# An encoder trunk: products of zeros on TensorE ahead of the first weights, and the state-space matrices fetched earlier

## The chip, the cores and the metric

One Trainium2 chip, one core of it. The metric is the device time of one execution in microseconds. Names of engines: TensorE is PE (its weight loads are PEld), VectorE is DVE, ScalarE is ACT, GpSimd is POOL, and SyncE is SP, whose queue only issues transfers here.

## The reference

A two-layer encoder on 256 tokens of width 1024, all in float32. Each layer adds half a SwiGLU block, a mixer of three branches and half a SwiGLU block again; a norm ends the trunk.

```python
for i in range(DEPTH):                                   # 2 layers
    h = rms_norm(x, ffn1_norm[i])
    x = x + 0.5 * (silu(h @ w_gate) * (h @ w_up)) @ w_down   # 1024 -> 2816 -> 1024
    h = rms_norm(x, mix_norm[i])
    ... = split(h @ w_in[i])                             # columns of three branches
    y_s5   = s5_branch(u, lambda, log_dt, b, c, d, w_glu)    # state space: bu = B_bar u, scan, C
    y_gla  = gla_branch(...)                             # gated linear attention
    y_attn = attn_branch(...)                            # attention with rotary positions
    gates  = sigmoid(h @ w_merge_gate[i] + b_merge_gate[i])
    x = x + (sum of gates * (y @ w_branch)) @ w_out[i]
    h = rms_norm(x, ffn2_norm[i])
    x = x + 0.5 * swiglu_ffn(h, ...)
return rms_norm(x, final_norm)
```

The state-space branch has complex matrices B and C (s5_b_re, s5_b_im, s5_c_re, s5_c_im; 2 directions, 32 groups, 64 states, 16 channels). Tables for it are made from B, C and the parameters lambda and log_dt.

## The kernel before

**Weights.** Every large product runs as three products of float32r parts (`mm3`, lines 234 to 236): the activation's high part by the weight's high part, by the weight's low part, and its low part by the weight's high part. `load` fetches weights in tiles of 128 x 2 x 512 (512 KB; for the gate and up matrices SP issues one transfer each, line 220), ScalarE casts the tile to hi (line 224), and VectorE subtracts to lo (line 225). The tiles `raw` rotate through 5 buffers, and so do hi and lo. The small vector tiles of `vectors` take a buffer of the `raw` ring too. A `raw` buffer is free again when its lo is made.

**Streaming.** `stream` walks over blocks of 512 output columns and chunks of 4 k-tiles (2 weight tiles). In `ffn` the first two blocks go side by side: step 0 is block 0 with the first chunk, step 1 block 1 with the first chunk, step 2 block 0 with the second, step 3 block 1 with the second, then two steps to a block. A weight tile is used by 12 products of 128x128 by 512 columns (2 k-tiles, 2 token tiles, 3 parts). The very first chunk is loaded in finer pieces (one k-tile each, `fine`).

**The norm.** `Norm.half` transposes half of x on TensorE (line 1158) and makes its high and low parts hTh and hTl; `ffn` calls `half(0)` ahead of the stream, and the hook of step 0 makes `half(1)`. In `__init__` x and the vector ffn1_norm are fetched first, with high priority; `vectors` transposes the vector (line 189).

**The tables.** `s5_tables` is a generator that `weave` interleaves with the feed-forward stream: in layer 0 from step 2 on with 1.8 of its parts to a step (PREP), in layer 1 from step 6 on with 0.85. Its first part fetches cst, three vectors (layer 0) and tcst. Then come `s5_params` (lambda as lm, log_dt as ld, lines 420 and 421, and some 17 parts of small VectorE work), `small_tables` (gla_norm, w_alpha as wraw, attn norms), and then B as bn (line 531, 4 transfers of 128 KB) and C as cn (line 537, 32 transfers of 16 KB in rows of 256 B). cn shares its memory with the scratch tiles U0 and U1, so the trace names it U. TensorE transposes cn (line 543, cT), and the rest builds the tables of four groups q.

**Order.** The program is traced in the order of the code, and a planner (`schedule_with_timeline_sim`) then fixes each engine's queue ahead of time, by its own estimate of when operands and buffers are ready; where several instructions are ready for an engine, the one that was traced first goes first. `high_priority()` without an offset puts instructions to the front; `load` uses it with an offset of 0 (WPRIO), so weight loads stand at their traced place. `behind` adds an order between two instructions of a queue without a wait; cst is tied so behind the last weight load. On the chip each queue is worked off strictly in its order.

Of the kernel before, what the change touches and what calls it, by code (L numbers as in the profile page):

```python
# [9 lines left out]
F32 = mybir.dt.float32  # L10
# [5 lines left out]
P = 128  # L16
# [66 lines left out]
def cols(*parts):  # L83

    def f(a, z):
        res, o = [], 0
        for w, cs in parts:
            res.append((w[a * P:z * P, cs].rearrange("(k p) n -> p k n", p=P), 0, o))
            o += cs.stop - cs.start
        return res  # L90
    return f
# [34 lines left out]
class Enc:  # L126
    def __init__(self, tc, ctx, ins, out):
        self.tc, self.nc, self.ctx, self.ins, self.out = tc, tc.nc, ctx, ins, out
        nc = self.nc
        pool = lambda name, bufs, **kw: ctx.enter_context(tc.tile_pool(name=name, bufs=bufs, **kw))  # L130
        self.const = pool("const", 1)
        self.wraw = pool("wraw", WBUFS[0])
        self.whl = pool("whl", WBUFS[1])
        self.hp = pool("hp", 1)
        self.st = pool("st", 2)
        self.pmm = pool("pmm", 3, space=bass.MemoryType.PSUM)
        self.psm = pool("psm", 3, space=bass.MemoryType.PSUM)
        self.ptr = pool("ptr", 2, space=bass.MemoryType.PSUM)
        self.n = self.ahead_by = 0
        c = self.const  # L140
        self.ident = c.tile([P, P], F32, name="ident")
        make_identity(nc, self.ident)
        self.x = c.tile([P, NT, D], F32, name="x")
        self.cst = c.tile([P, C_MIX], F32, name="cst")
        self.row = {}
        self.mhalf = c.tile([P, 32], F32, name="mhalf")
        nc.gpsimd.memset(self.mhalf, -0.5)

        nc.scalar.activation(c.tile([P, 1], F32, name="warm"), self.mhalf[:, :1], AF.Silu)
        with tc.high_priority():  # L150
            xd = lambda eng, t, h: eng.dma_start(self.x[:, t, h * 512:(h + 1) * 512],
                                                 ins["x"][0, t * P:(t + 1) * P, h * 512:(h + 1) * 512])
            xd(nc.scalar, 0, 0)
            xd(nc.sync, 1, 0)
            self.vectors("ffn1_norm", eng=nc.scalar)
            for t in range(NT):
                xd(nc.scalar, t, 1)
        self.ld = pool("s5ld", 1)
        self.ahead, self.small = {}, {}
        self.scr = {(l, q): tc.dram_tile([P, SCR], F32, name=f"scr{l}_{q}") for l in range(DEPTH) for q in range(NQ)}  # L160
# [4 lines left out]

    def t2(self, shape, dt=F32, ring="ra"):
        return self.phase.tile(shape, dt, name=self.nm("t"), tag=ring, bufs=self.rings[ring])

    def vectors(self, *names, eng=None):

# [108 lines left out]
    def ffn(self, l, which, nm, nxt):  # L279

        nc, ins = self.nc, self.ins
        wg, wu, wd = (ins[f"{which}_w_{s}"][l] for s in ("gate", "up", "down"))
        with self.tc.tile_pool(name=f"ffn{which}{l}", bufs=1) as fp:
            self.phase, self.rings = fp, {"ra": 4}
            if nm.at == 0:
                nm.half(0)
            act, rstd = nm.act, nm.rstd
            sh = fp.tile([P, KF, SEQ], F32R, name=f"sTh{which}{l}")
            sl = fp.tile([P, KF, SEQ], F32R, name=f"sTl{which}{l}")

            def evac(b):
                def f(t, ps):
                    self.n += 1
                    sg, s = self.t2([P, 256]), self.t2([P, 256])
                    nc.scalar.activation(sg, ps[:, :256], AF.Silu, scale=rstd[:, t:t + 1])  # L295
                    nc.vector.scalar_tensor_tensor(s, ps[:, 256:], rstd[:, t:t + 1], sg, op0=ALU.mult, op1=ALU.mult)  # L296
                    pt = self.ptr.tile([P, 2, P], F32, name=f"st{self.n}", tag="tr")
                    for j in range(2):
                        nc.tensor.transpose(pt[:, j], s[:, j * P:(j + 1) * P], self.ident)  # L299
                    h = sh[:, 2 * b:2 * b + 2, t * P:(t + 1) * P]  # L300
                    nc.scalar.copy(h, pt)  # L301
                    nc.vector.tensor_tensor(sl[:, 2 * b:2 * b + 2, t * P:(t + 1) * P], pt, h.bitcast(F32),  # L302
                                            op=ALU.subtract)
                return f

            blocks = []
            for b in range(KF // 2):
                cs = slice(b * 256, (b + 1) * 256)
                blocks.append((cols((wg, cs), (wu, cs)), 512, evac(b)))
            yield from self.stream(act, KD, blocks, lead=2, hooks={0: nm.finish}, fine=(l, which) == (0, "ffn1"))  # L310
            nm2 = self.nxt = nxt()
            last = isinstance(nm2, Final)

            def down(c):
                def f(t, ps):
                    xs = self.x[:, t, c * 512:(c + 1) * 512]
                    nc.vector.scalar_tensor_tensor(xs, ps, 0.5, xs, op0=ALU.mult, op1=ALU.add)
                    if last:
                        nm2.half(c, t)
                return f  # L320

            sact = lambda k, t: (sh[:, k, t * P:(t + 1) * P], sl[:, k, t * P:(t + 1) * P])
            yield from self.stream(sact, KF, [(cols((wd, slice(c * 512, (c + 1) * 512))), 512, down(c))
                                              for c in range(2)],
                                   hooks=() if last else {-(-KF // WCH) + 1: lambda: nm2.half(0)},
                                   tail=3 * WCH if last else None)
# [183 lines left out]
    def s5_tables(self, l, pp):  # L510
        nc, ins = self.nc, self.ins
# [3 lines left out]
            self.vectors("mix_norm", "ffn2_norm", "s5_d")  # L515
        self.tcst = pp.tile([P, C_ALL - C_MIX], F32, name="tcst")
        nc.sync.dma_start(self.tcst, ins["cst"][:, C_MIX:])
        yield
        yield from self.s5_params(l, pp)
        yield  # L520
        self.small_tables(l, pp)
        yield
        b = []
        T2 = [pp.tile([P, GQ, 64], F32, name=f"U{i}") for i in range(4)]
        cn = [T2[i].rearrange("p g c -> p (g c)").rearrange("p (t r) -> p t r", t=4) for i in range(2)]
# [1 line left out]
        for i, s in enumerate(("re", "im")):  # L527
            bn = pp.tile([P, G, 16], F32, name=self.nm("bn"))
            b.append(bn)
            for d in range(2):  # L530
                nc.sync.dma_start(bn[d * 64:(d + 1) * 64], ins[f"s5_b_{s}"][l, d].rearrange("g p f -> p g f"))
            for d in range(2):
                for e in range(2):
                    for h in range(2):
                        for ii in range(2):
                            r = e * 64 + h * 32 + ii * 16
                            nc.sync.dma_start(
                                cn[i][r:r + 16, :, d * 64:(d + 1) * 64],
                                ins[f"s5_c_{s}"][l, d].rearrange("(h q i e) f p -> e h i f q p", q=NQ, e=2, h=2)[e, h, ii])
        for i in range(2):  # L540
            ps = self.psm.tile([P, 4, P], F32, name=self.nm("cT"), tag="sm")
            for t in range(4):
                nc.tensor.transpose(ps[:, t], cn[i][:, t], self.ident)
            nc.scalar.copy(cq[:, i], ps)
            if i == 1:
                nc.scalar.activation(cq[:, 2], ps, AF.Copy, scale=-1.0)
        yield
        T = [pp.tile([P, GQ, 4, 16], F32, name=f"T{i}") for i in range(4)]
        for q in (1, 2, 3, 0):
# [14 lines left out]
            for i in range(2):  # L564
                ps = self.psm.tile([P, 4, P], F32, name=self.nm("bT"), tag="sm")
# [15 lines left out]
            for i in range(2):  # L581
                for a in range(4):
                    for d in range(2):
# [3 lines left out]
                                         start=i == 0, stop=i == 1)  # L587
# [545 lines left out]
class Norm:  # L1133
# [14 lines left out]
        return self.hi[:, k, ts], self.lo[:, k, ts]  # L1148

    def half(self, c):  # L1150
        e, nc = self.e, self.e.nc
        self.at = c + 1
        for j in range(2):
            pt = e.ptr.tile([P, 2, SEQ], F32, name=e.nm("pt"), tag="tr")
            for i in range(2):
                k = 4 * c + 2 * j + i
                for t in range(NT):
                    nc.tensor.transpose(pt[:, i, t * P:(t + 1) * P], e.x[:, t, k * P:(k + 1) * P], e.ident)
            for i in range(2):
                k = 4 * c + 2 * j + i  # L1160
                g, h = self.g[:, k:k + 1], self.hi[:, k]
                nc.scalar.activation(h, pt[:, i], AF.Copy, scale=g)  # L1162
                nc.vector.scalar_tensor_tensor(self.lo[:, k], pt[:, i], g, h.bitcast(F32), op0=ALU.mult, op1=ALU.subtract)
        for t in range(NT):
            nc.scalar.activation(e.t2([P, 512]), e.x[:, t, c * 512:(c + 1) * 512], AF.Square,
                                 accum_out=self.sq[:, c, t:t + 1])

    def finish(self):
        e, nc = self.e, self.e.nc
# [89 lines left out]
```

## Time and profile before

| | |
|---|---|
| Median of 3 runs | 1335.75 us (1334.98 to 1336.29) |
| Profiled execution | 1336.15 us, span of its instructions 1334.4 us |
| TensorE products | 1299.3 us busy, 97% of the span |
| VectorE, ScalarE, GpSimd | 75%, 52%, 6% of the span |
| Transfers | 249.87 MB, mean 187 GB/s |

The profile is of one execution; times in it count from the start of its span. Products are pipelined: one that is shown with 0.39 us can follow the one before it after 0.23 us, so the distance of starts tells the pace. A row of the time axis that ends in x2 or more merges instructions of one kind that follow each other. A bracket at its end says how long the engine was idle before it and what ended that.

### The profile page before, as it was taken

To read this page: it belongs to the slowest core of one execution; us is meant where nothing else is said; L and a number is where in the kernel's file an instruction comes from. 1 tells how busy PE (TensorE), PEld (TensorE's weight loads), DVE (VectorE), ACT (ScalarE), POOL (GpSimd) and SP (SyncE) were. 2 spreads that over 40 slices of the span, in tenths; PEclk is the share of its full clock that TensorE was granted. 3 is DMA by queue.
4 is the path that set the end of the run, shared out by engine and by line. 5 is a ranking of instruction groups with operands and counts; after the bars stand their busy time and mean duration, and the time that the engine had idled before them with its cause. 6 is when DMAs were issued, how large, how long until landed. Compare 5 with 4: busy or idle time off the path is not lost.

```text
span 1334.4 us, 19260 instructions
## 1 busy us (share of the span) xinstructions
PE 1299.3 (97%) x6792; PEld 1049.9 (79%) x6792; DVE 1001.1 (75%) x1798; ACT 699.8 (52%) x1132; POOL 81.2 (6%) x109
## 2 busy tenths in 40 slices
PE   8999999999999999999999999999999999999997
PEld 6788878878787777888888778887787867788886
DVE  5899896789996778997576757557899966655553
ACT  6454455547685445544454454463485853655442
POOL 1022211000100000101010000000001000000000
PEclk9999999999999999999999999999999999999999
DMA  8775686765463457677656565576655525555661
GB/s 254 180 216 162 228 299 193 208 230 192 155 195 111 127 162 198 193 250 233 189 168 210 180 221 182 172 201 203 193 192 185 177 65 173 165 181 186 194 204 63
DMA packets 201264, 249.87 MB, mean 187 GB/s; under 512 B 40920, under 2 KB 134664, under 8 KB 201168
## 3 DMA queue, kind: packets, MB, share of 16 engines
q1 hardware_dynamic: 200416, 247.33, 59.5%
q8 instruction: 53, 0.87, 0.3%
q10 hardware_dynamic: 752, 1.32, 0.3%
q14 instruction: 43, 0.35, 0.1%
HBM read 234.44 MB, written 13.11 MB: 186 GB/s over the span
## 4 chain that ended last, share of the span: by engine, by line
PE 74%; DVE 13%; DMA 5%; issue 4%; POOL 2%; SPq 1%; ACT 1%; POOLq 0%; ACTq 0%; DVEq 0%
PE mm L234 22%; PE mm L236 22%; PE mm L235 22%; DVE lo L225 3%; DMA e<-scr 2%; DMA raw<-in_ffn_w_up 2%; DVE t L330 2%; POOL kx L610 1%; PE st L299 1%; DVE run L823 1%; PE as L1057 1%; PE ao L1079 1%; PE S L805 1%; DVE run L822 1%; ACT hi L224 1%
## 5 line engine op out<-in xcount | busy, mean ns | idle before, releaser
L225 DVE TENSOR_TENSOR lo<-raw,hi 128x1024 fp32r<-128x1024 f32 (+2 forms) x414 | 498.9, 1209 | 190.3 <-ACT hi L224 184.5
L224 ACT CAST hi<-raw 128x1024 fp32r<-128x1024 f32 (+2 forms) x414 | 428.6, 1039 | 339.5 <-PE mm L236 271.4
L234 PE MATMUL mm<-hi,hTh 128*128 128x512 f32 (+1 forms) x1120 | 441.2, 396 | 4.9 <-ACT hTh L1162 2.6
L235 PE MATMUL mm<-lo,hTh 128*128 128x512 f32 (+1 forms) x1120 | 440.8, 395 | 3.3 <-DVE lo L225 3.0
L236 PE MATMUL mm<-hi,hTl 128*128 128x512 f32 (+1 forms) x1120 | 431.0, 392 | 0.0
L234 PEld LDWEIGHTS mm<-hi,hTh 128*128 128x128 f32 x1120 | 211.5, 189 | 48.6 <-ACT hTh L1162 3.1
L235 PEld LDWEIGHTS mm<-lo,hTh 128*128 128x128 f32 x1120 | 211.3, 189 | 45.4 <-DVE lo L225 5.1
L236 PEld LDWEIGHTS mm<-hi,hTl 128*128 128x128 f32 x1120 | 210.9, 189 | 40.9
L235 PE MATMUL mm<-lo,sThffn 128*128 128x512 f32 x352 | 137.6, 391 | 0.9 <-DVE lo L225 0.9
L236 PE MATMUL mm<-hi,sTlffn 128*128 128x512 f32 x352 | 137.5, 392 | 0.0
L234 PE MATMUL mm<-hi,sThffn 128*128 128x512 f32 x352 | 136.5, 393 | 0.7 <-ACT hi L224 0.7
L235 PEld LDWEIGHTS mm<-lo,sThffn 128*128 128x128 f32 x352 | 66.1, 188 | 15.1 <-DVE lo L225 1.6
L234 PEld LDWEIGHTS mm<-hi,sThffn 128*128 128x128 f32 x352 | 66.1, 188 | 14.6 <-ACT hi L224 1.1
L236 PEld LDWEIGHTS mm<-hi,sTlffn 128*128 128x128 f32 x352 | 66.1, 188 | 14.2
L295 ACT ACTIVATE t<-mm,rstd 128x256 f32<-128x256 f32 x88 | 41.2, 474 | 52.8 <-PE mm L236 50.7
L301 ACT CAST sThffn<-st 128x256 fp32r<-128x256 f32 x88 | 31.4, 372 | 68.5 <-PE st L299 68.1
L302 DVE TENSOR_TENSOR sTlffn<-st,sThffn 128x256 fp32r<-128x256 f32 x88 | 35.7, 417 | 35.5 <-ACT sThffn L301 35.5
L296 DVE SCALAR_TENSOR_TENSOR t<-mm,rstd,t 128x256 f32<-128x256 f32 x88 | 40.7, 477 | 11.7 <-ACT t L295 11.5
L610 POOL COPY kx<-ks 128x128 f32<-128x128 f32 x32 | 28.1, 919 | 231.0 <-DVE ks L593 187.0
L299 PE MATMUL st<-ident,t 128*128 128x128 f32 x176 | 31.7, 274 | 1.6 <-DVE t L296 0.8
L299 PEld LDWEIGHTS st<-ident,t 128*128 128x128 f32 x176 | 23.4, 140 | 11.9 <-DVE t L296 1.3
L330 DVE TENSOR_TENSOR t<-e,S 128x512 f32<-128x512 f32 x32 | 20.3, 682 | 15.1 <-DMA e<-scr 12.5
(355 smaller groups left out, 1411.5 us busy)
## 6 DMA issues: line engine op xcount, KB each, us to landing
raw<-in_ffn_w_down SPq DMA_DIRECT2D x88, 512.0 KB, 4.6
raw<-in_ffn_w_gate SPq DMA_DIRECT2D x174, 256.0 KB, 2.8
raw<-in_ffn_w_up SPq DMA_DIRECT2D x174, 256.0 KB, 3.8
raw<-in_w_in SPq DMA_DIRECT2D x48, 512.0 KB, 4.9
raw<-in_w_merge_gate SPq DMA_DIRECT2D x48, 512.0 KB, 4.5
raw<-in_w_out SPq DMA_DIRECT2D x16, 512.0 KB, 4.9
scr<-e SPq DMA_DIRECT2D x6, 768.0 KB, 8.2
e<-scr SPq DMA_DIRECT2D x6, 768.0 KB, 6.4
```

The costliest lines, as they stand in the source:

```text
L224: nc.scalar.copy(hi[:, j:z, :width], raw[:, j:z, :width])
L225: nc.vector.tensor_tensor(lo[:, j:z, :width], raw[:, j:z, :width], hi[:, j:z, :width].bitcast(F32), op=ALU.subtract)
L234: nc.tensor.matmul(ps, act[0], w[0], start=first, stop=False)
L235: nc.tensor.matmul(ps, act[0], w[1], start=False, stop=False)
L236: nc.tensor.matmul(ps, act[1], w[0], start=False, stop=last)
L295: nc.scalar.activation(sg, ps[:, :256], AF.Silu, scale=rstd[:, t:t + 1])
L296: nc.vector.scalar_tensor_tensor(s, ps[:, 256:], rstd[:, t:t + 1], sg, op0=ALU.mult, op1=ALU.mult)
L299: nc.tensor.transpose(pt[:, j], s[:, j * P:(j + 1) * P], self.ident)
L301: nc.scalar.copy(h, pt)
L302: nc.vector.tensor_tensor(sl[:, 2 * b:2 * b + 2, t * P:(t + 1) * P], pt, h.bitcast(F32), op=ALU.subtract)
L330: self.nc.vector.tensor_tensor(out, a, b, op=ALU.mult)
L610: nc.gpsimd.tensor_copy(kx[:, :, s], ks.rearrange("p g j f -> p g (j f)")[:, :, (3 - s) * 16:(3 - s) * 16 + 64])
```

## The change

A tile of zeros is made on VectorE. `idle(n)` issues n products of this tile with itself (128x128, float32) into a PSUM tile of the ring `mm` that nobody reads. 11 of them are traced at the head of `__init__`, with high priority, and 8 in the first `ffn`, each behind the last transpose of `half(0)`, which now returns it. In `s5_tables` the fetches of B and C are moved from behind `small_tables` to the first part, behind tcst; the transposes of C stay where they were. The number of parts is the same.

```diff
--- before.py
+++ after.py
@@ -147,7 +147,11 @@
         nc.gpsimd.memset(self.mhalf, -0.5)
 
         nc.scalar.activation(c.tile([P, 1], F32, name="warm"), self.mhalf[:, :1], AF.Silu)
+
+        self.zero = c.tile([P, P], F32, name="zero")
+        nc.vector.memset(self.zero, 0.0)
         with tc.high_priority():
+            self.idle(11)
             xd = lambda eng, t, h: eng.dma_start(self.x[:, t, h * 512:(h + 1) * 512],
                                                  ins["x"][0, t * P:(t + 1) * P, h * 512:(h + 1) * 512])
             xd(nc.scalar, 0, 0)
@@ -165,6 +169,14 @@
 
     def t2(self, shape, dt=F32, ring="ra"):
         return self.phase.tile(shape, dt, name=self.nm("t"), tag=ring, bufs=self.rings[ring])
+
+    def idle(self, n, prev=None):
+
+        ps = self.pmm.tile([P, 512], F32, name=self.nm("idle"), tag="mm")
+        for _ in range(n):
+            m = self.nc.tensor.matmul(ps[:, :P], self.zero, self.zero, start=True, stop=True)
+            if prev is not None:
+                self.behind(m, prev)
 
     def vectors(self, *names, eng=None):
 
@@ -283,7 +295,7 @@
         with self.tc.tile_pool(name=f"ffn{which}{l}", bufs=1) as fp:
             self.phase, self.rings = fp, {"ra": 4}
             if nm.at == 0:
-                nm.half(0)
+                self.idle(8, nm.half(0))
             act, rstd = nm.act, nm.rstd
             sh = fp.tile([P, KF, SEQ], F32R, name=f"sTh{which}{l}")
             sl = fp.tile([P, KF, SEQ], F32R, name=f"sTl{which}{l}")
@@ -515,11 +527,6 @@
             self.vectors("mix_norm", "ffn2_norm", "s5_d")
         self.tcst = pp.tile([P, C_ALL - C_MIX], F32, name="tcst")
         nc.sync.dma_start(self.tcst, ins["cst"][:, C_MIX:])
-        yield
-        yield from self.s5_params(l, pp)
-        yield
-        self.small_tables(l, pp)
-        yield
         b = []
         T2 = [pp.tile([P, GQ, 64], F32, name=f"U{i}") for i in range(4)]
         cn = [T2[i].rearrange("p g c -> p (g c)").rearrange("p (t r) -> p t r", t=4) for i in range(2)]
@@ -537,6 +544,11 @@
                             nc.sync.dma_start(
                                 cn[i][r:r + 16, :, d * 64:(d + 1) * 64],
                                 ins[f"s5_c_{s}"][l, d].rearrange("(h q i e) f p -> e h i f q p", q=NQ, e=2, h=2)[e, h, ii])
+        yield
+        yield from self.s5_params(l, pp)
+        yield
+        self.small_tables(l, pp)
+        yield
         for i in range(2):
             ps = self.psm.tile([P, 4, P], F32, name=self.nm("cT"), tag="sm")
             for t in range(4):
@@ -1148,6 +1160,7 @@
         return self.hi[:, k, ts], self.lo[:, k, ts]
 
     def half(self, c):
+
         e, nc = self.e, self.e.nc
         self.at = c + 1
         for j in range(2):
@@ -1155,7 +1168,7 @@
             for i in range(2):
                 k = 4 * c + 2 * j + i
                 for t in range(NT):
-                    nc.tensor.transpose(pt[:, i, t * P:(t + 1) * P], e.x[:, t, k * P:(k + 1) * P], e.ident)
+                    last = nc.tensor.transpose(pt[:, i, t * P:(t + 1) * P], e.x[:, t, k * P:(k + 1) * P], e.ident)
             for i in range(2):
                 k = 4 * c + 2 * j + i
                 g, h = self.g[:, k:k + 1], self.hi[:, k]
@@ -1164,6 +1177,7 @@
         for t in range(NT):
             nc.scalar.activation(e.t2([P, 512]), e.x[:, t, c * 512:(c + 1) * 512], AF.Square,
                                  accum_out=self.sq[:, c, t:t + 1])
+        return last
 
     def finish(self):
         e, nc = self.e, self.e.nc
```

## Rows read from the trace of the kernel before

**Rows 1.** The page, busy time: us (share of span) x instructions

```profile
PE 1299.3 (97%) x6792; PEld 1049.9 (79%) x6792; DVE 1001.1 (75%) x1798; ACT 699.8 (52%) x1132; POOL 81.2 (6%) x109
```

**Rows 2.** Waits of TensorE, whole span: us in total, times, longest

```profile
PE mm L235 <- DVE lo L225: 3.9, 3, 1.5
...
PE cT L543 <- DMA U<-in_s_c_re: 0.7, 1, 0.7
...
PE cT L543 <- DMA U<-in_s_c_im: 0.3, 1, 0.3
```

**Rows 3.** Time axis of the opening: start, duration, engine, line, output<-input

```profile
5.71 1.97 PE L1158 MATMUL pt<-ident,x 128*128 128x128 f32 x8
...
8.46 1.22 PE L234 MATMUL mm<-hi,hTh 128*128 128x512 f32 x2 [0.78 <-ACT hi L224]
...
9.48 0.63 PE L235 MATMUL mm<-lo,hTh 128*128 128x512 f32 x1
...
9.91 0.63 PE L236 MATMUL mm<-hi,hTl 128*128 128x512 f32 x1
...
17.94 0.48 PE L235 MATMUL mm<-lo,hTh 128*128 128x512 f32 x1
...
18.73 0.40 PE L235 MATMUL mm<-lo,hTh 128*128 128x512 f32 x1
...
18.96 0.39 PE L236 MATMUL mm<-hi,hTl 128*128 128x512 f32 x1
```

**Rows 4.** Busy time by stretch: PE, PEld, DVE, ACT, POOL, clock, DMA, GB/s

```profile
8.50:14.30 5.80, 5.80 (x14) 4.51 (x15) 4.03 (x9) 3.28 (x8) 1.25 (x1) 1.00 0.90 266
17.90:28.40 10.50, 10.50 (x49) 8.69 (x48) 6.80 (x10) 5.96 (x9) 0.00 (x0) 1.00 0.78 237
```

**Rows 5.** TensorE by line, 8.4 to 28.3 us: count, busy, mean ns, idle

```profile
L236 PE MATMUL mm<-hi,hTl 128*128 128x512 f32 x24 | 10.0, 430 | 0.0
```

**Rows 6.** SP's queue, time axis, 0 to 24 us

```profile
1.19 0.42 SPq L517 DMA_DIRECT2D tcst<-in_cst  x1
...
15.73 2.47 SPq L181 DMA_DIRECT2D vec<-in_s_d  x4
18.73 0.40 SPq L220 DMA_DIRECT2D raw<-in_ffn_w_gate  x1
...
21.75 0.42 SPq L421 DMA_DIRECT2D ld<-in_s_log_dt  x1
22.27 0.38 SPq L220 DMA_DIRECT2D raw<-in_ffn_w_gate  x1
```

**Rows 7.** Time axis, the splits of weight tiles r3, r5 and r7

```profile
15.39 1.22 DVE L225 TENSOR_TENSOR lo<-raw,hi 128x1024 fp32r<-128x1024 f32 x1 [2.40 <-ACT hi L224]
...
18.36 1.22 DVE L225 TENSOR_TENSOR lo<-raw,hi 128x1024 fp32r<-128x1024 f32 x1 [0.26 <-ACT hi L224]
...
22.40 1.05 ACT L224 CAST hi<-raw 128x1024 fp32r<-128x1024 f32 x1 [1.54 <-DMA raw<-in_ffn_w_up]
```

**Rows 8.** SP's queue, time axis, 24 to 60 us

```profile
26.04 0.47 SPq L628 DMA_DIRECT2D gn<-in_gla_norm  x1
...
39.49 3.29 SPq L531 DMA_DIRECT2D bn<-in_s_b_re  x2
...
58.95 2.15 SPq L531 DMA_DIRECT2D bn<-in_s_b_im  x2
```

**Rows 9.** TensorE on the time axis, 245 to 251 us

```profile
246.76 1.95 PE L805 MATMUL S<-U,bb 128*128 128x128 f32 x16
248.54 1.04 PE L697 MATMUL qkT<-ident,t 128*128 128x128 f32 x8
```

**Rows 10.** SP's queue, time axis, layer 1

```profile
480.57 0.34 SPq L517 DMA_DIRECT2D tcst<-in_cst  x1
...
498.68 2.81 SPq L537 DMA_DIRECT2D U<-in_s_c_re  x6
...
516.36 7.54 SPq L537 DMA_DIRECT2D U<-in_s_c_im  x12
```

## The prediction

> **What bounds the kernel now.** I began with the page's busy times: TensorE is busy 97% of the span [rows 1]. So a gain must shorten TensorE's products or one of its gaps, and a loss must open a new gap. The waits of TensorE [rows 2] list the gaps: 0.7 and 0.3 us in front of the transposes of the state-space matrix C (tile U in the trace, cn in the code), waiting for C's own transfers, and waits for splits, the longest of them 1.5 us.
>
> Then I read the opening on the time axis [rows 3]. TensorE does 8 transposes of x from 5.71 us, in 1.97 us. The first product starts at 8.46, when the first hi is cast, and the third at 9.48, when its lo is there. From there the products are back to back, but slowly: 9.91 follows 9.48 by 0.43 us and each lasts 0.63 us, while 18.73 and 18.96, later in the same stage, are 0.23 apart and last 0.40. The stretch from 8.5 to 14.3 holds 14 such products [rows 4]. Its granted clock stands at 1.00, as in the stretch behind it, so that column doesn't show the difference; 512 columns in 0.43 us are the 1.2 GHz level, and 0.23 us is near the 2.4 GHz level. Until 5.71 TensorE had next to nothing to do, and then transposes and slow products went ahead of the faster pace.
>
> Last came SP's queue, which issues the weights, and this decides. Call the 512 KB weight tiles r1, r2, ... in load order (r1 and r2 come in four fine pieces). In the stretch after the first six tiles [rows 6], SP issues cst, two vectors and four s5_d pieces, which end at 18.20, then r7 (18.73), r8, lm, lm, ld, then r9. That is the traced order: s5_tables traces cst, the vectors and s5_d behind ffn's step 2 and ahead of step 3, whose loads are r7 and r8. It holds though the buffers were free before: r7's buffer was released when r3's split ended at 16.61 (15.39 + 1.22) and r9's when r5's did at 19.58 (18.36 + 1.22) [rows 7], and yet s5_d and the lm/ld loads went first. So a small load traced earlier keeps its place ahead of a weight load that is ready. Small loads traced later only fill holes: gla_norm, traced some ten steps on, comes at 26.04, and B and C from 39.49 on [rows 8]. One load stands far ahead of its traced place, tcst at 1.19, in front of r1 [rows 6]: a hole that took one load and no second, though lm was free to go too.
>
> **The zeros, part by part.** They add one memset at the very start (nothing waits for it but the zeros), two PSUM tiles written by TensorE alone, and 19 products of 128x128 f32. Such products run 16 in 1.78 us at the full pace, 246.76 to 248.54 [rows 9], so 0.11 us each; at half pace I take 0.21 to 0.25 (0.11 times 0.43/0.23; the opening transposes, 1.97/8 [rows 3]). The first 11 take 2.3 to 2.8 us and wait for nothing but the memset, so they lie inside the idle time ahead of 5.71. The other 8 stand between the transposes and the first product: at half pace 1.7 to 2.0 us from 7.68, so to about 9.5, and the first product slips by 1.0; at full pace 0.9, hidden under the wait for the first hi. What they could return is the slow opening: 14 products at 0.43 instead of 0.23 us are 2.8 us. But TensorE would then meet the weights: r3's lo is there at 16.61 [rows 7], a time that the transfers set; the products that need it start at 17.94 [rows 3] and could start no earlier than about 16.85, when the order around them is kept. That makes 1.1 us the likeliest gain, between a loss of 1.0 and a gain of 2.8.
>
> **The moved fetch.** Removed: C's late arrival, 0.7 + 0.3 = 1.0 us of TensorE [rows 2]; nothing else there waits for it. Moved: in each layer 4 transfers of B and 32 of C, now traced with tcst, in the first side step. In layer 0 that is behind step 2 and so ahead of r7. By the order just read, SP issues all 36 between s5_d and r7. Their price on SP: B takes 3.29 us for one pair and 2.15 for the other [rows 8], 5.4 together; C takes 0.47 each in a run of six and 0.63 in a run of twelve [rows 10], so 15.0 to 20.1 for 32. I take the middle, 17.5, since layer 0's own mixture lies there, and 23.0 in all (20.4 to 25.5). From 18.20 that puts r7 at 41.2 instead of 18.73: 22.5 us late (19.9 to 25.0).
>
> What hides it: TensorE has r1 to r6 in store. Up to 28.3 us it does exactly 72 products, 24 on each of its three lines and 12 for each of six tiles [rows 5], so it turns to r7 at 28.5. r7's hi was cast by 23.45 (22.40 + 1.05) [rows 7], a cover of 5.05 us. The rest is a gap: 22.5 - 5.05 = 17.5 us (14.9 to 20.0), ending near 46. An earlier end of the first six tiles only makes the gap begin earlier, so in this case the zeros' gain counts for nothing. Queued behind the moved loads on SP are r7, r8, lm and ld, every later weight, and then the parameters and small tables. ScalarE and VectorE have nothing to split meanwhile. The parameters come as late as the weights, so their distance to the mixer stays.
>
> After the gap, does the slow pace come back? No row of before shows a gap of that length; the longest that it waited for a lo is 1.5 us [rows 2]. The nearest row is the opening, where TensorE came out of idleness at half pace for 14 products [rows 3, 4], so 2.8 us; the bound below is nothing. I take 2.8. The Trainium skill (TensorE: Matmul & The Clock Gate, Part 1) says that an array without work is throttled to half its pulses again, which would make it 2.8 too, where an end of the effect after the opening would make it 0.
>
> Layer 1: there SP has holes. tcst is issued at 480.57 and C from 498.68 to 524 between weight loads [rows 10], well ahead of the steps that trace them (step 7 and step 27 of a stage that has hardly begun then). Weight loads of steps 0 to 7 are traced ahead of the moved loads and pass them; the 36 fill the holes that the small tables filled, and lm comes some 30 us later, long before the mixer. I price that at 0 (-1 to +1).
>
> **Sum**, against the profiled execution (1336.15 us, span 1334.4; 0.4 above the median): 1336.15 + 17.5 + 2.8 - 1.0 = 1355.5, less 0.4: 1355.1. With every term at its kind end, layer 1's among them: 1336.15 + 14.9 - 1.0 - 1.0 - 0.4 = 1348.7; at the other end 1336.15 + 20.0 + 2.8 + 1.0 - 1.0 - 0.4 = 1358.6.
>
> **The rivals.**
> *The moved loads are hidden after all* (the other side). If the planner sees r7 as ready while it deems SP free and puts the weights first, the 36 fill holes as before, and what is left is C's 1.0 and the opening's 1.1: 1336.15 - 2.1 - 0.4 = 1333.7 (1332 with the whole 2.8, 1336 if the zeros don't lift the pace and hold the first product by 1.0). For it: in before the very same loads, from 39.49 to 76, cost TensorE nothing but the 1.0. Against it: r7 and r9 behind small loads though their buffers were free. It decides where no more than about eight of the moved loads get ahead of r7 (5.05 us at 0.6). The Trainium skill (DMA: Bandwidth & Descriptors, Rules for kernel authors) advises to issue a DMA early, compute and wait late; by that rule this rival is the case. It presumes that nothing more urgent stands behind the early DMA, which the weights here are [rows 6].
> *Half of them*: one of the two matrices (18 loads, 11.5 us) gets ahead of r7 and the other doesn't: a gap of 11.5 - 5.05 = 6.5, less 1.0 and 0.4, 1341.
> *The zeros do nothing*, since a product of zeros doesn't lift the pace or the wait behind the first eleven undoes it: under the gap that changes nothing, and with a hidden fetch the time is 1336.15 - 1.0 - 0.4 = 1334.8, or 1335.8 where they hold the first product.
>
> **How the numbers follow.** The full queue block has a chance of 0.55, half of it 0.10, the hidden fetch 0.35. Two runs of this kernel can be told apart from about 0.2%, 2.7 us. The hidden fetch gives 1332 to 1336, of which I put 0.15 below 1333.1 and 0.20 within 0.2%; the other two cases are slower, 0.65. I predict the likeliest, 1355, with an own range of 1348 to 1359 (the two ends above). For 8 in 10 the range has to take in the half block and most of the hidden cases: 1333 to 1359.
>
> **What would show it.** Right: SP's queue with bn and U ahead of the third step's weights, r7 issued near 41 us; one TensorE gap of 15 to 20 us that ends near 46, with ScalarE's hi waiting for raw; products at over 600 ns behind it; C's two waits gone; 19 more TensorE instructions with zero. Wrong: r7 still issued near 19 us, a cover longer than the 5 us that I read, or several of the moved loads beside tcst ahead of r1, where each would hold the first products themselves. The zeros are judged by the duration of the products from 8.4 to 14.4 us: near 390 they work, near 620 they don't.

## The result

The changed kernel takes 1357.88 us (median of 4 runs, 1355.96 to 1359.51) beside 1336.02 for the kernel before on the same chip: 1.0167 times as long, interval 1.0152 to 1.0183. The forecast was 1355, slower. The profiled execution took 1359.27 us, its span is 1357.4, so 23.1 more than before's 1334.4. Line numbers are each kernel's own; in the changed one most stand 12 higher than before (L246 to L248 are the products L234 to L236).

SP's queue of the changed kernel on the time axis (start, duration, queue, line), beside [rows 6, 8]:

```profile
15.34 2.49 SPq L193 DMA_DIRECT2D vec<-in_s_d  x4
18.30 1.93 SPq L538 DMA_DIRECT2D bn<-in_s_b_re  x2
20.28 8.39 SPq L544 DMA_DIRECT2D U<-in_s_c_re  x16
28.71 1.81 SPq L538 DMA_DIRECT2D bn<-in_s_b_im  x2
30.56 8.69 SPq L544 DMA_DIRECT2D U<-in_s_c_im  x16
39.35 0.39 SPq L232 DMA_DIRECT2D raw<-in_ffn_w_gate  x1
```

All 36 loads stand between s5_d and r7, which is issued at 39.35 instead of 18.73. They take 20.8 us of SP (the four durations): 0.52 to 0.54 for each load of C, 1.8 to 1.9 for each pair of B.

TensorE on the time axis, the opening and the gap, beside [rows 3]; in brackets the idle time before a row and what ended it:

```profile
1.05 5.06 PE L177 MATMUL idle<-zero 128*128 128x128 f32 x22 [1.05 <-DVE zero L152]
...
6.26 1.29 PE L1171 MATMUL pt<-ident,x 128*128 128x128 f32 x8
7.39 1.95 PE L177 MATMUL idle<-zero 128*128 128x128 f32 x16
9.10 0.71 PE L246 MATMUL mm<-hi,hTh 128*128 128x512 f32 x2
...
26.75 0.39 PE L248 MATMUL mm<-hi,hTl 128*128 128x512 f32 x1
...
44.18 1.22 PE L246 MATMUL mm<-hi,hTh 128*128 128x512 f32 x2 [15.34 <-ACT hi L236]
45.72 0.31 PE L437 MATMUL lmT<-ident,lm 32*128 32x32 f32 x1 [0.32 <-DMA lm<-in_s_lambda_re]
46.03 1.09 PE L555 MATMUL cT<-ident,U 128*128 128x128 f32 x4
...
48.31 0.63 PE L246 MATMUL mm<-hi,hTh 128*128 128x512 f32 x1
48.74 0.63 PE L247 MATMUL mm<-lo,hTh 128*128 128x512 f32 x1
```

Each product of zeros shows as two instructions, 22 for the eleven and 16 for the eight; the eleven take 5.06 us, the eight 1.7 (7.39 to 9.10). The transposes behind the first zeros take 1.29 us where they took 1.97 [rows 3]. The six tiles end at 26.75, against some 28.3 before. Then the gap, 15.34 us. Behind it the products stand 0.43 us apart, and TensorE has 0.50 of its clock granted, the 1.2 GHz level, as the busy times by stretch say (PE, PEld, DVE, ACT, POOL, clock, DMA, GB/s):

```profile
28.40:44.00 15.60, 0.44 (x3) 0.15 (x2) 0.72 (x3) 1.29 (x2) 0.00 (x0) 0.57 0.47 98
44.00:51.00 7.00, 6.50 (x17) 4.51 (x18) 4.23 (x5) 3.75 (x5) 0.00 (x0) 0.50 0.98 292
51.00:60.00 9.00, 9.00 (x41) 7.14 (x40) 8.26 (x25) 5.01 (x7) 1.12 (x1) 1.00 1.05 329
```

The two waits for C are gone from TensorE's waits, whose first rows are now (in all, times, longest; beside [rows 2]):

```profile
PE mm L246 <- ACT hi L236: 16.4, 2, 15.3
PE mm L247 <- DVE lo L237: 6.8, 6, 1.8
```

In layer 1, which I had priced at nothing, the small tables' loads come late (agq at 547.18 instead of 489.18 us), and ScalarE sits idle for 8.95 us in front of the cast that reads one of them (wraw), with casts of hi behind it. ScalarE, then TensorE, on the time axis:

```profile
549.34 1.05 ACT L650 CAST wa<-wraw 96x1024 fp32r<-96x1024 f32 x1 [8.95 <-DMA agq<-in_attn_q_norm]
550.29 0.63 ACT L313 CAST sThffn<-st 128x256 fp32r<-128x256 f32 x2
550.82 2.95 ACT L236 CAST hi<-raw 128x1024 fp32r<-128x1024 f32 x3
```

```profile
542.60 0.50 PE L247 MATMUL mm<-lo,hTh 128*128 128x512 f32 x1 [1.24 <-DVE lo L237]
...
555.43 0.50 PE L247 MATMUL mm<-lo,hTh 128*128 128x512 f32 x1 [1.83 <-DVE lo L237]
...
558.55 0.63 PE L248 MATMUL mm<-hi,hTl 128*128 128x512 f32 x1
```

### The profile page after: what moved, and what is told of

It reads as the page before. It is cut to its first block, busy times and chain, and to the rows that moved or that the text cites. A ratio compares the mean times of both kernels' runs of the same rounds, so it can differ in the third digit from the quotient of the medians.

```text
span 1357.4 us, 19334 instructions
## 1 busy us (share of the span) xinstructions
PE 1308.7 (96%) x6830; PEld 1057.7 (78%) x6830; DVE 1001.6 (74%) x1799; ACT 698.9 (51%) x1132; POOL 92.4 (7%) x109
## 4 chain that ended last, share of the span: by engine, by line
PE 72%; DVE 13%; DMA 5%; SPq 4%; issue 4%; POOL 1%; ACT 1%; POOLq 0%; DVEq 0%; ACTq 0%
PE mm L246 21%; PE mm L248 21%; PE mm L247 21%; DVE lo L237 4%; DMA raw<-in_ffn_w_up 2%; SPq L544 2%; DVE t L342 1%; SPq L232 1%; PE st L311 1%; POOL e L612 1%; PE S L817 1%; DMA raw<-in_ffn_w_down 1%; DMA e<-scr 1%; PE ao L1091 1%; DVE run L835 1%
## 5 line engine op out<-in xcount | busy, mean ns | idle before, releaser
L236 ACT CAST hi<-raw 128x1024 fp32r<-128x1024 f32 (+2 forms) x414 | 427.9, 1038 | 343.8 <-PE mm L248 265.5
L246 PE MATMUL mm<-hi,hTh 128*128 128x512 f32 (+1 forms) x1120 | 441.3, 396 | 19.7 <-ACT hi L236 15.3
L248 PE MATMUL mm<-hi,hTl 128*128 128x512 f32 (+1 forms) x1120 | 429.7, 391 | 0.0
L246 PEld LDWEIGHTS mm<-hi,hTh 128*128 128x128 f32 x1120 | 210.9, 189 | 63.0 <-ACT hi L236 15.5
L248 PEld LDWEIGHTS mm<-hi,hTl 128*128 128x128 f32 x1120 | 211.0, 189 | 41.1
L248 PE MATMUL mm<-hi,sTlffn 128*128 128x512 f32 x352 | 138.2, 393 | 0.0
L246 PE MATMUL mm<-hi,sThffn 128*128 128x512 f32 x352 | 136.6, 394 | 1.0 <-ACT hi L236 1.0
L246 PEld LDWEIGHTS mm<-hi,sThffn 128*128 128x128 f32 x352 | 66.5, 189 | 15.1 <-ACT hi L236 1.5
L248 PEld LDWEIGHTS mm<-hi,sTlffn 128*128 128x128 f32 x352 | 66.4, 189 | 13.9
L308 DVE SCALAR_TENSOR_TENSOR t<-mm,rstd,t 128x256 f32<-128x256 f32 x88 | 40.7, 477 | 15.7 <-ACT t L307 15.4
L622 POOL COPY kx<-ks 128x128 f32<-128x128 f32 x32 | 28.5, 932 | 228.8 <-DVE ks L605 228.0
L612 POOL TENSOR_TENSOR e<-r,tcst 128x512 f32<-128x512 f32 x8 | 23.7, 2960 | 196.8 <-DVE r L342 126.9
```

Source lines behind the costliest of these rows:

```text
L236: nc.scalar.copy(hi[:, j:z, :width], raw[:, j:z, :width])
L246: nc.tensor.matmul(ps, act[0], w[0], start=first, stop=False)
L248: nc.tensor.matmul(ps, act[1], w[0], start=False, stop=last)
L612: nc.gpsimd.tensor_tensor(ld["e"][:, SCR_R - SCR_E:].rearrange("p (g c) -> p g c", g=GQ), self.r4[:, gs].unsqueeze(2).to_broadcast((P, GQ, ...
L622: nc.gpsimd.tensor_copy(kx[:, :, s], ks.rearrange("p g j f -> p g (j f)")[:, :, (3 - s) * 16:(3 - s) * 16 + 64])
```

## The experiments

The table sets each run's profiled execution against before's, at the starts of the 72nd, 640th, 1010th, 1800th and 2200th of the big products, those of 256 columns or more on the full 128x128 array (before: 28.5, 174.0, 272.3, 507.8 and 605.1 us; counted from 0, so the 72nd is the first that needs r7): the us gained or lost in each stretch. Other TensorE work can slip across a mark, so single stretches are good to one or two us; large entries and the sum count. The ratio is that of timed runs to the kernel before, with its interval.

```
run         ratio [interval]          to 72  -640 -1010 -1800 -2200   end    sum
after       1.0167 [1.0152, 1.0183]   +15.7  +2.2  +1.9  -1.0  +5.8  -1.4  +23.1
move_only   1.0168 [1.0154, 1.0181]   +15.1  +0.2  +1.3  -1.3  +7.0  +0.2  +22.5
move_l0     1.0137 [1.0121, 1.0153]   +15.2  +1.2  +2.1  +0.8  +0.0  -0.2  +19.0
move_l1     1.0039 [1.0024, 1.0054]    -0.1  +0.3  -1.3  -0.9  +7.6  -0.7   +4.9
zeros_only  1.0002 [0.9991, 1.0014]    -1.6  +0.4  +1.3  +0.5  -0.1  -0.3   +0.3
half_l0     1.0081 [1.0066, 1.0096]    +4.8  -0.9  +5.0  +2.3  -0.1  -0.6  +10.6
gap_zeros   1.0186 [1.0162, 1.0210]   +16.4  +1.6  -0.2  -1.0  +6.1  +0.3  +23.1
act_queue   1.0149 [1.0123, 1.0175]   +15.9  +4.4  -2.0  +2.2  -0.8  +0.3  +20.1
zeros_mid   1.0082 [1.0064, 1.0100]    -1.4  +9.5  -0.7  +1.1  +5.6  -1.7  +12.5
l1_tables   1.0021 [1.0009, 1.0033]    -0.9  +0.2  +0.2  +0.7  -0.4  +4.5   +4.4
zeros_r     0.9998 [0.9986, 1.0010]    -1.2  -1.7  -4.2  +8.5  -0.4  -0.9   +0.2
before_r    0.9991 [0.9982, 1.0000]    -0.6  -0.2  -4.2  +5.8  -0.4  +0.1   +0.6
after_r     1.0174 [1.0158, 1.0191]   +15.3  +1.3  -4.2  +4.9  +5.9  +0.9  +24.2
```

**The change taken apart.** `move_only` is the moved fetch without zeros, `move_l0` and `move_l1` the same in one layer alone (the fetch stands early `if l == 0`, or `if l == 1`), `zeros_only` the zeros with the fetch at its old place:

```
         self.small_tables(l, pp)
         yield
+        [the fetch of B and C]
```

> The moved fetch in both layers, without any zeros. My theory: the gap begins later but ends at the same time, since it ends when the third step's weights land; so this runs as the changed kernel does, 1356 to 1359, with r7 issued near 39 us and one gap of about 16 us from 28.3 to near 44. Rival: the zeros' gain survives the gap, then it is 1.5 slower than the changed kernel; second rival: the zeros make part of the loss (they delay the first product by 0.6 us), then it is faster than 1356.

> The fetch moved in layer 0 alone, no zeros. My theory: the queue block of layer 0 makes most of the loss, 17.5 us as the two traces show it at the 432nd product, so 1336 + 17.5 = 1353 to 1354; what is missing to the changed kernel's 1358 is layer 1's, about 5. Rival: layer 1 costs nothing, as I forecast, and the difference came from layer 0's later course (the gap at 209 to 215 us): then this runs at 1356 to 1359.

> The fetch moved in layer 1 alone, no zeros. My theory: layer 1 loses by itself, since lm and ld come 56 us later there (537 instead of 481) and the agq and ld that VectorE waits for at 541 to 551 come late: two gaps and a slow stretch of TensorE between 540 and 567, +4 to +6, so 1340 to 1342. Rival: layer 1 is free as I forecast (-1 to +1): 1335 to 1337, and the +6 in the changed kernel is a consequence of the weights' lateness since layer 0.

> The zeros (11 and 8 products) as in the changed kernel, with the fetch of B and C back at its old place. My theory: the zeros themselves win. In the changed kernel the product that ends the first six weight tiles came 1.5 us earlier than before (26.75 instead of 28.28), so without the queue block the time is that of before less 1.5: about 1334.5, ratio 0.999, and the products in the opening stand 0.23 us apart from about 10.9 on. Rival: the gain was only the gap's doing (nothing behind it shows it) or the zeros hold the first product for nothing: 1336 to 1337.

The move alone costs as much as the whole change (1.0168 beside 1.0167). Layer 0 costs 18.3 us (0.0137 of 1336) and layer 1 5.2; together 23.5, beside 22.4 for both at once. So layer 1 isn't free, and my pricing of it falls. In the trace of `move_only` the gap begins later and is shorter (14.09 us, ended by hi at 43.57), as a gap must that ends with the weights.

The zeros alone change nothing (1.0002), and my expectation of -1.5 failed. They do what they are for: the products stand 0.23 us apart from the first ones on, and at the 600th product the kernel is 1.9 us ahead of the one before. Part of that is one execution's chance: the runs without zeros don't open alike (13 products at half pace in before and `half_l0`, 6 to 9 in the others), and beside `move_l1`, whose layer 0 is that of before, the lead is 0.5. Most of it goes around 190 us. First GpSimd, then VectorE, then TensorE of `zeros_only` there:

```profile
169.80 12.81 POOL L612 TENSOR_TENSOR e<-r,tcst 128x512 f32<-128x512 f32 x1 [13.24 <-DMA scr<-e]
```

```profile
181.63 0.68 DVE L329 SCALAR_TENSOR_TENSOR x<-mm,x 128x512 f32<-128x512 f32 x1
187.75 0.69 DVE L362 TENSOR_TENSOR e<-U,U 128x512 f32<-128x512 f32 x1 [5.44 <-DMA scr<-e]
188.35 1.53 DVE L366 TENSOR_TENSOR e<-U,U 128x512 f32<-128x512 f32 x1
...
189.97 0.68 DVE L329 SCALAR_TENSOR_TENSOR x<-mm,x 128x512 f32<-128x512 f32 x1
```

```profile
190.70 0.99 PE L1171 MATMUL pt<-ident,x 128*128 128x128 f32 x7 [1.26 <-DVE x L329]
192.13 0.51 PE L247 MATMUL mm<-lo,sThffn 128*128 128x512 f32 x1 [0.44 <-DVE lo L237]
...
193.25 0.63 PE L247 MATMUL mm<-lo,sThffn 128*128 128x512 f32 x1
```

GpSimd's product for tile e takes 12.81 us. VectorE works without a break until 182.31 (181.63 + 0.68), GpSimd ends at 182.61, and SP issues the store of e at 182.64. VectorE's next write of e must wait for that store; x and lo stand behind it in VectorE's queue, and TensorE waits for both and then runs at half pace. The waits alone aren't the loss, for TensorE is idle 2.4 us in the stretch from the 640th to the 1010th product and was idle 2.7 us before; the eight products at half pace cost 1.6 us. Before, GpSimd's product took 1.21 us:

```profile
171.12 1.21 POOL L600 TENSOR_TENSOR e<-r,tcst 128x512 f32<-128x512 f32 x1 [12.14 <-DMA scr<-e]
```

There VectorE was the one held up; its row beside that product (rows of this kind last 0.68 us):

```profile
171.35 1.53 DVE L347 TENSOR_TENSOR T<-cq,lpc 128x512 f32<-128x512 f32 x1
```

So the two engines seem to hold each other up. The Trainium skill (SBUF — State Buffer, SBUF: two separate sides) states that VectorE and GpSimd share a pair of ports as an exclusive lock, over which a VectorE instruction with two inputs in SBUF and a GpSimd instruction that reads SBUF contend, and that the one who starts first holds it for its whole instruction. The 1.53 us agree with that. The 12.81 us don't follow from it: 19 instructions of VectorE, not one, ran between 169.72 and 182.31, and GpSimd's product ended 0.30 us behind the last. Why it got no turn between them isn't shown; no run here looked at the port itself.

**That product on VectorE.** Three runs move it: `zeros_r` with the zeros alone, `before_r` without any change, `after_r` with all of it.

```
-            nc.gpsimd.tensor_tensor(ld["e"][:, SCR_R - SCR_E:]...
+            v.tensor_tensor(ld["e"][:, SCR_R - SCR_E:]...
```

> The zeros alone (fetch at its old place), and the product that makes the third part of tile e from r and tcst runs on VectorE instead of GpSimd (8 instructions of 0.68 us more on VectorE). My theory: the zeros' gain of 1.9 us at the 600th product was given back at 190 us, where GpSimd's product met VectorE's back-to-back work and took 12.8 us instead of 1.2, so that scr came late and VectorE waited 5.4 us; with the product on VectorE it isn't given back: 1334 to 1335, about 2 below the same kernel without zeros. Rival: the loss at 190 us has another cause (the weights' slots): 1336 to 1337, as the zeros alone.

> The control for the run above: the kernel before with that one product on VectorE. There GpSimd's products took 1.2 to 4.9 us and nothing waited for them, so 1336 to 1337 by my theory. Rival: the move to VectorE is itself a gain or a loss of over 1 us.

> The changed kernel with that one product on VectorE. My theory: the 1.9 us that the changed kernel lost between the 640th and the 1010th product (one product of 13.3 us on GpSimd, then a gap and 8 products at half pace) goes away, 1355.5 to 1356.5. Rival: the collision is only a symptom, and the time stays at 1357.5 to 1359.

The place is confirmed: in all three TensorE has no idle time between the 640th and the 1010th product and none of the products at half pace, where `zeros_only` lost 1.3 us, and the stretch is 4.2 us shorter. Of the 4.2, 2.7 are idle time that the kernel before has there too, and about 0.9 are eight small products that slip behind the mark. But nothing is left of it at the end (0.9998, 0.9991, 1.0174): in the next stretch, which holds layer 0's mixer, 4.9 to 8.5 us come back. `zeros_r` leads `before_r` by 2.3 us at the 1446th product (393.6 beside 396.0 us) and trails it by 0.3 at the 1538th (423.7 beside 423.4). TensorE's instructions stand in another order there once that product is moved, so that the stretches don't compare step by step. Part of what takes the lead away is in the trace, though. TensorE of `zeros_r`, then its busy times by stretch (columns as above):

```profile
385.96 0.69 PE L1013 MATMUL goT<-ident,t 128*128 128x128 f32 x2 [1.55 <-ACT aqT L1057]
...
389.31 0.41 PE L887 MATMUL glu<-ysl,hi 128*128 128x256 f32 x1
389.52 0.41 PE L888 MATMUL glu<-ysh,lo 128*128 128x256 f32 x1
```

```profile
385.00:395.00 10.00, 8.49 (x47) 7.82 (x48) 7.73 (x17) 4.87 (x12) 0.00 (x0) 0.66 0.36 105
```

From 383 to 388 us TensorE waits three times, 2.7 us in all (2.9 in `before_r` and `after_r`), where the kernel before doesn't wait at all from 357 to 425 us. Behind these waits some 20 products of 256 columns stand 0.21 us apart (some 25 in `before_r`, 12 in `after_r`); in all other runs they stand 0.12 apart. That is about 2 us in `zeros_r`. Over the whole stretch TensorE's idle time grows by only 1.2 to 1.8 us, since an earlier wait gets shorter. Why the order came out so, and what takes the rest, stays open. My expectations for `zeros_r` and `after_r` failed.

**Is it the order on SP, and how large?** `half_l0` moves only the real halves of B and C in layer 0 (18 loads). `act_queue` issues the 36 loads from ScalarE's queue, in the changed kernel's place:

```
-                nc.sync.dma_start(bn[d * 64:(d + 1) * 64], ...
+                nc.scalar.dma_start(bn[d * 64:(d + 1) * 64], ...
```

> No zeros; in layer 0 only the real halves of B and C (18 loads) are fetched ahead of the third step's weights, the imaginary halves and all of layer 1 stay at the old place. My theory (the loss is SP's issue time of the loads ahead of r7, less a cover of about 5): 18 loads take 10.2 to 10.4 us on SP at the changed kernel's prices (1.93 and 8.39 for the real halves), so r7 comes about 10.3 late, a gap of 10.3 - 5.05 = 5.3, and 2 to 2.8 for the slow pace behind it: 1336 + 7.3 to 8.1, less 0.5 for the C that is no longer late: 1343. Rival (the loss is proportional to the loads moved, no cover): half of 18.5, 1345.5. Rival (a fixed price for any gap): 1353.

> The changed kernel with the 36 loads of B and C in each layer issued from ScalarE's queue instead of SP's, in the same traced place. My theory (the loss is SP's order of issue): r7 is issued near 17 to 19 us as before and the gap of TensorE is gone. ScalarE now spends 20.8 us on issuing between its casts of hi; its hi would come late by a few issues (0.52 each), so small waits are possible: 1336 to 1340. Rival (the 36 transfers, 2048 packets of 64 bytes for each B, burden the DMA engines wherever they are issued from): the weights r3 to r8 land as late as in the changed kernel, 1350 to 1358.

SP's queue and TensorE of `half_l0`:

```profile
20.14 8.41 SPq L535 DMA_DIRECT2D U<-in_s_c_re  x16
28.65 0.39 SPq L220 DMA_DIRECT2D raw<-in_ffn_w_gate  x1
```

```profile
33.31 1.22 PE L234 MATMUL mm<-hi,hTh 128*128 128x512 f32 x2 [3.30 <-ACT hi L224]
```

r7 comes 9.9 us late (28.65 beside 18.73) and the first product that needs it 4.8, so the cover is 5.1: the rule holds. The whole came out at 10.8 us (0.0081), not 7.3 to 8.1; 5.0 of it lies between the 640th and the 1010th product, where that product on GpSimd took 12.76 us and TensorE waited 4.08 for lo at 191.72.

`act_queue` missed all that I expected of it. SP is free for the weights, and r7 goes out at 24.23, yet the gap ends near 44 again. ScalarE's own row says why; ACTq is its queue of issues:

```profile
33.25 8.94 ACTq L544 DMA_DIRECT2D U<-in_s_c_im  x11
42.31 4.83 ACT L236 CAST hi<-raw 128x1024 fp32r<-128x1024 f32 x5 [8.71 <-DMA wraw<-in_gla_b_alpha]
```

Eleven issues in a row hold ScalarE for 8.94 us, and the cast of hi starts behind them. The weights for it were issued 17 to 18 us before that (24.23, 25.23), and by the trace's semaphores they had landed at 31.1, so the rival, that the transfers themselves hold up the weights, has no support. But the 8.94 us aren't the price of issuing. The eleven issues (shortest, median and longest in ns, first and last start), and their loads from issue to landing:

```profile
L544 ACTq DMA_DIRECT2D U<-in_s_c_im x11: 317/318/438, 33.3 to 41.8; - x11
DMA to landing us min/median/max: 1.5/3.5/4.0
```

Eleven issues of 0.32 to 0.44 us make some 4 us; in the other 5 ScalarE waits ahead of an issue. The loads in this queue take turns with four semaphores, and an issue waits until the load four before it has landed: the one at 37.27 follows a landing at 37.25, the one at 40.92 a landing at 40.90. SP's loads of C in the changed kernel take turns with eight semaphores and follow each other every 0.47 us. So the block is paid on whichever engine issues in order, on SP as time of issue, on ScalarE more than half as waits for landings. What the issuing alone would cost on ScalarE no run shows.

**The half pace behind the gap.** `gap_zeros` is the changed kernel with 76 more products of zeros behind the last product of step 2's tiles.

> The changed kernel with 76 more products of zeros behind the last product of step 2's tiles, which fill the gap of TensorE (26.75 to 44.18) with 16.2 us of work at the full pace (0.107 us for each of 152 instructions). My theory: the slow pace behind the gap comes from the idleness, so now the products from 44.2 on stand 0.23 us apart instead of 0.43 (12 to 14 of them until 51.2), and the time falls by 2.2 to 2.8 against the changed kernel: 1355.2. The gap in useful work stays. Rival: the slow pace belongs to that stretch (the weights' arrival, late lo) and not to the idleness: 1357 to 1359 as the changed kernel.

```profile
30.67 14.01 PE L177 MATMUL idle<-zero 128*128 128x128 f32 x124
...
46.16 0.50 PE L247 MATMUL mm<-lo,hTh 128*128 128x512 f32 x1 [0.76 <-DVE lo L237]
...
46.73 0.39 PE L246 MATMUL mm<-hi,hTh 128*128 128x512 f32 x1
46.96 0.39 PE L247 MATMUL mm<-lo,hTh 128*128 128x512 f32 x1
```

The half pace is gone (0.23 us apart from 46.73), so it did come from the idleness. The Trainium skill (TensorE: Matmul & The Clock Gate, Part 1) states that an array without work falls to half its pulses, and this run agrees: 0.23 us behind the filled gap, 0.43 behind the empty one. At the 88th product `gap_zeros` is 3.1 us ahead of the changed kernel. At the 160th it is 1.2 behind: the weights come no earlier, and TensorE's idle time from the 72nd to the 180th is 3.4 us instead of 1.0. The time doesn't fall (1.0186). The mechanism was right, but as a term of the sum it is worth nothing here.

**Layer 1, and a middle place.** `zeros_mid` traces the fetch behind the parameters and ahead of the small tables, in both layers. `l1_tables` has no zeros and leaves layer 0 alone; in layer 1 the order is small tables, fetch, parameters.

```
+        if l == 1:
+            self.small_tables(l, pp)
+            [the fetch of B and C]
+            yield
         yield from self.s5_params(l, pp)
```

> The zeros of the changed kernel, and the fetch of B and C traced behind the state-space parameters and ahead of the small tables, in both layers: behind the third step's weights, and behind lm and ld. My theory: no queue block in layer 0 (r7 near 18 us) and none in layer 1, where lm and ld keep their time; C arrives earlier than in before, which returns its two waits (1.0): 1334.5 to 1336. What the zeros gain in the opening (1.9 at the 600th product in the run of the zeros alone) may again be given back at 190 us, where a product of tile r on GpSimd took 12.8 us instead of 1.2. Rival: layer 1's loss came from the place of B and C behind the weights and stays at +4: 1340.

> Layer 0 as before, no zeros. In layer 1 the fetch of B and C is moved ahead of the parameters as in the changed kernel, but the small tables (wraw, agq, agk) are traced ahead of it. My theory: layer 1's loss is ScalarE's: the cast of wa, which waits for the small tables' loads, stands in its queue ahead of casts of hi, and behind the moved fetch those loads come late (ScalarE sat idle for 9 to 10 us in front of that cast in all three runs that lost in layer 1). With the tables first the cast finds its data, and the time is that of before: 1335 to 1338. Rival: the loss is that of the parameters (lm and ld 34 to 56 us later, VectorE's copy of lm waiting 8.6 us): then it stays, 1340 to 1342.

`zeros_mid` ended two theories: layer 0 has no queue block any more (-1.4 to the 72nd product) and yet loses 9.5 us by the 640th, and layer 1 loses 5.6 though lm and ld are issued first. Both losses have the same sign in ScalarE's queue; layer 0's, and TensorE's wait that follows from it:

```profile
73.44 1.04 ACT L650 CAST wa<-wraw 96x1024 fp32r<-96x1024 f32 x1 [10.69 <-DMA wraw<-in_gla_w_alpha]
74.39 0.63 ACT L313 CAST sThffn<-st 128x256 fp32r<-128x256 f32 x2
74.92 2.94 ACT L236 CAST hi<-raw 128x1024 fp32r<-128x1024 f32 x3
```

```profile
76.02 0.79 PE L246 MATMUL mm<-hi,hTh 128*128 128x512 f32 x1 [6.28 <-ACT hi L236]
80.89 0.80 PE L247 MATMUL mm<-lo,hTh 128*128 128x512 f32 x1 [2.58 <-DVE lo L237]
```

`l1_tables` tells the two readings of layer 1 apart. With the tables first, the stretch to the 2200th product costs nothing (-0.4 instead of +7.6). But the parameters are late in it, and 4.5 us go in the last stretch. GpSimd, then TensorE:

```profile
636.00 7.33 POOL L608 TENSOR_TENSOR e<-r,tcst 128x512 f32<-128x512 f32 x1 [33.97 <-DMA scr<-e]
```

```profile
651.01 0.80 PE L235 MATMUL mm<-lo,sThffn 128*128 128x512 f32 x1 [2.56 <-DVE lo L225]
```

It is the wait of 190 us once more. That the late parameters bring it is not shown: in `move_l1` they are late too (lm at 515.09, here at 524.84), and its last stretch loses nothing (-0.7). What is shown is the first reading: with the small tables ahead of the fetch, the loss in front of the 2200th product is gone. `act_queue` agrees, where the fetch doesn't stand in SP's queue: there the cast of wa waits 1.14 us, and the stretch loses nothing (-0.8). `before_r` comes nearest to beating the kernel before (0.9991), within what can't be told from no change.

## Why the prediction came out right, and where it was off

*The queue block* was the step that decided, and it held: the 36 loads ahead of r7, a cover of 5.05, a gap that the zeros can't shorten. It was mis-sized: 23.0 us for the loads, 20.8 measured, so r7 at 39.35 instead of 41.2. The delay at the 72nd product is 15.7 instead of 17.5 (20.6 late less 5.05 is 15.6). Too dear were the pairs of B, which I took from loads issued between weights, 2.15 and 3.29 [rows 8]; in a block they take 1.9.

*The half pace* behind the gap appeared as forecast, for about 7 us at 0.50, but the 2.8 don't reach the end (`gap_zeros`). *C's waits* went away as forecast; their 1.0 can't be seen apart. Layer 0 as a whole, 17.5 + 2.8 - 1.0 = 19.3 in the forecast, measured 18.3 with the move alone: near, partly by luck, since the later stretches (+1.2, +2.1 and +0.8 in `move_l0`) make up what the 2.8 was to give.

*Layer 1* is the step that failed. I followed the moved loads and lm, found holes for them, and priced the stretch at 0; it costs 5.2 alone. (Nor was the hole for lm where I put it: it came 56 us later, 537.27 beside 480.97, not some 30.) I had named the parameters and small tables as queued behind the loads, but not their readers: ScalarE's cast of wa and VectorE's work on agq, which stand among the splits of weights. That the whole still came within 3 us of the forecast is partly luck: these 5.2 stand against a queue block priced 1.8 too high and a half pace that doesn't reach the end.

*The zeros* were mispriced. I took an instruction in [rows 9] for a product; a product is two, so eleven took 5.06 us instead of 2.3 to 2.8 and the first product slipped by 0.6 (9.10 beside 8.46; in `zeros_only` they took 4.51, and it didn't slip, 8.44). Still the six tiles ended 1.5 us earlier, near the 1.1 forecast, and the gap swallowed it as forecast. With the fetch hidden I'd have given them that 1.1; alone they measure nothing, because most of the lead is lost around 190 us.

*The rivals.* The hidden fetch didn't happen: no load went ahead of r1 but tcst, none filled a hole behind it in layer 0. The half block I had put at 1341; built by hand it takes 1347, since the same later stretch adds 5.

## What to carry to other kernels

In layer 0 a block of small loads on SP delayed TensorE by its count times the issue time, less the work already in store (15.6 us reckoned, 15.7 measured; 4.8 for half the loads). Moved to another engine's queue, the same block held up that engine's work instead, partly by waits for earlier loads to land. When loads slip in a queue, list the readers of everything behind them: one late cast in an in-order queue stops the splits that follow it. A lead won in the opening counts only if every later chain that paces the kernel moves with it, so a gain is to be followed through the trace to the end.

## What the runs showed that was not expected

One and the same product on GpSimd took from 1.21 us (before) to 12.81 (`zeros_only`) and 13.34 (the changed kernel), with VectorE busy all through. It isn't the zeros as such: it took 13.86 in `move_l0`, without them, and 1.56 in `gap_zeros`, where it started 0.7 us later than in the changed kernel (189.64 beside 188.90). Short gaps of TensorE were enough for the half level in one place and not in another: in the changed kernel the products behind 1.83 us of waiting at 555.43 soon stood 0.43 apart, up to 559.4, while behind 1.24 us at 542.60, and behind 1.79 us at 270.94 in the kernel before, they stayed at 0.23. And a load of C took 0.32 us (median) to issue from ScalarE, 0.42 from SP, yet in a row of eleven ScalarE got through one only every 0.81 us.
